# One conformer-attention layer on one core: token tile 0 starts the next stage at both ends, and vector work there in written order

## The chip, the cores and the metric

One core of one Trainium2 chip runs the kernel. The metric is the device time of a whole execution in microseconds (us); lower is better. TensorE is PE in the profile, VectorE DVE, ScalarE ACT, SyncE SP; SP issues every large transfer.

## What is computed

One layer on 256 tokens of 2048 channels, all in float32: a half-step SwiGLU FFN, a token mixing (convolution on one group of channels, differential attention on the other), a second half-step FFN. Each is normalised before and after, and shifted, scaled and gated by nine vectors that are products of a conditioning vector with `w_ada` (2048 x 18432), called adaLN here.

```python
mod = (silu(c) @ w_ada[l] + b_ada[l])
sh1, sc1, gt1, sh2, sc2, gt2, sh3, sc3, gt3 = split(mod, 9)

h = rms_norm(x, g_pre[0]) * (1 + sc1) + sh1
x = x + 0.5 * gt1 * rms_norm(swiglu(h, w_gate1, w_up1, w_down1), g_post[0])

h = rms_norm(x, g_pre[1]) * (1 + sc2) + sh2
u_conv, q, k, v = split(h @ w_in)
y_conv = silu(layer_norm(causal_conv31(glu(u_conv))))
y_attn = rms_norm(diff_attention(q, k, v))
x = x + gt2 * rms_norm(concat(y_conv, y_attn) @ w_out, g_post[1])

h = rms_norm(x, g_pre[2]) * (1 + sc3) + sh3
x = x + 0.5 * gt3 * rms_norm(swiglu(h, w_gate2, w_up2, w_down2), g_post[2])
```

## The kernel before

The 256 tokens are two token tiles of 128 (`NT`), the 2048 channels sixteen chunks of 128 (`NK`, index `kt`). A float32 number is split into a high part that TensorE multiplies exactly and a low part, the rest; every product is three matmuls, high by high, high by low, low by high (`mm3`, L270; blocks of the convolution and of the q and k projections do the same with the weights as the stationary operand).

Weights come in blocks of 1 MB. `load` (L151) issues the transfer on SP's queue into one of four raw buffers, `parts` (L156) makes the high part by a cast on ACT (L160) and the low part by a subtraction on DVE (L162), with three buffers for the results. An adaLN product (`ada_chunk`, L180) is a transfer of 1 MB into the same four raw buffers and one DVE pass over it (L183). There are 144 of them, and they are drawn from a generator (`bg`) wherever the code asks for one: in the fronts of the first FFN, then one for every `EVERY1` weight blocks (`tick`), then in the token mixing and in the front of the second FFN (`late`, one for every `LATE` chunks).

The order of the instructions on each engine is fixed when the kernel is built, by the tile scheduler, except inside a region of `manual_schedule`, where DVE and ACT keep the order in which the code is written (before, that is only the start of the kernel).

The stages in order: four fronts of the first FFN (`MFront`, `first_front`), each cut in four groups of chunks; its remaining gate and up blocks (`wgu`) and down blocks (`wd`); the first end; the convolution's blocks (`Front`, L290), which begin the token mixing; the q and k projections, with the softmax and the convolution's taps (L630) between them; the values (`values`, L718) with the attention products (`mix_values`, L725); the output projection, by heads (`of_heads`) and by convolution channels (`of_conv`); the second end; the second FFN.

An end is where a stage closes. `m_last` (L418) runs the last two units of the output (512 channels each): all products of tile 0, then all of tile 1. `evac` adds the bank to the sum (L486), squares it for the mean (L236) and multiplies by the gate (L489); `close` (L253) normalises the sum, adds it to x (L260) and calls `normed` (L238), which scales x for the next stage (L245 on ACT, L247 on DVE). Then `front_of` (L558) transposes the scaled x chunk by chunk, both tiles at once (`pre_norm`, L212; transposes L218, shift and scale L222 or L225, high part L227, low part L228), and goes on with the next stage's blocks two chunks behind.

The convolution's result is centred and normalised (`center`, L787, `normalize`, L800; L808 sums squares, L811 and L813 invert the root, L818 scales) and split (L173 cast on ACT, L175 subtraction on DVE). The code asks for two adaLN products (`MIXC`) at each of the four output units.

## Time and profile before

| what | value |
|---|---|
| time, median of 3 runs | 1916.03 us (1913.0 to 1920.33) |
| profiled execution, its own time | 1911.84 us |
| its span in the profile | 1910.0 us |
| PE busy | 1836.3 us, 96% |
| DVE busy | 1423.6 us, 75% |
| ACT busy | 821.4 us, 43% |
| DMA | 492.58 MB, mean 258 GB/s |

Times of the trace count from the span's start. A busy share is an average over the stages, which differ: the fronts and the first FFN last to about 774 us, the token mixing to about 1150, the second FFN to the end. The kernel's runs lie within 0.4% of each other.

### The profile page before, as it was taken

The numbers are of one execution on the slowest core, as the hardware profiler recorded it, in microseconds if no ns is written. First come the engines' busy times: TensorE is split into PE (matmuls) and PEld (weight loads), VectorE is DVE, ScalarE is ACT, GpSimd is POOL, SyncE is SP. The second block draws the span as 40 slices with busy tenths as digits, with TensorE's granted clock in tenths as the row PEclk, the third lists the DMA queues.
The fourth block names the chain that finished last, engine by engine and source line by source line (L and its number), as shares of the span: only waits on it lengthen the run. The fifth ranks groups of instructions, "written<-read, shape, count | busy, mean of one in ns | idle before, by whom it ended". The sixth has DMA issues, their size and how long they took to land.

```text
span 1910.0 us, 22064 instructions
## 1 busy us (share of the span) xinstructions
PE 1836.3 (96%) x8944; PEld 1542.5 (81%) x8944; DVE 1423.6 (75%) x1594; ACT 821.4 (43%) x852; POOL 6.0 (0%) x49
## 2 busy tenths in 40 slices
PE   5999999999999999799998897999999999999997
PEld 3788888888888888699997686788888888888886
DVE  7789999788889888688998967854555555555455
ACT  4544445433433334643554454544344333343342
POOL 0000000000000000000000000000000000000000
PEclk9999999999999999899999898999999999999999
DMA  9888877989999998355444665865665666565552
GB/s 362 320 317 330 337 278 290 358 345 361 357 357 370 349 367 323 122 182 185 157 174 157 242 241 202 331 238 205 236 220 205 235 220 226 215 235 210 194 193 72
DMA packets 68934, 492.58 MB, mean 258 GB/s; under 512 B 7648, under 2 KB 7776, under 8 KB 9440
## 3 DMA queue, kind: packets, MB, share of 16 engines
q1 hardware_dynamic: 68832, 491.17, 69.0%
q8 instruction: 70, 1.15, 0.2%
q14 instruction: 32, 0.26, 0.0%
HBM read 489.05 MB, written 2.10 MB: 257 GB/s over the span
## 4 chain that ended last, share of the span: by engine, by line
PE 89%; DVE 5%; ACT 3%; DMA 2%; issue 0%; SPq 0%; DVEq 0%; ACTq 0%
PE ps L273 29%; PE ps L274 29%; PE ps L272 28%; DVE lo L162 2%; DMA raw<-in_wgu 2%; ACT hi L160 1%; DVE raw L183 1%; PE ps L413 1%; ACT tmp L236 1%; PE ps L312 0%; PE ps L311 0%; DMA raw<-in_wk 0%; PE ps L313 0%; PE ps L678 0%; PE ps L218 0%
## 5 line engine op out<-in xcount | busy, mean ns | idle before, releaser
L162 DVE TENSOR_TENSOR lo<-raw,hi 128x2048 fp32r<-128x2048 f32 x314 | 718.5, 2290 | 359.8 <-ACT hi L160 359.1
L160 ACT CAST hi<-raw 128x2048 fp32r<-128x2048 f32 x314 | 600.3, 1912 | 732.4 <-PE ps L274 362.0
L272 PE MATMUL ps<-hi,big 128*128 128x512 f32 x2256 | 879.2, 395 | 16.9 <-ACT big L227 11.3
L273 PE MATMUL ps<-lo,big 128*128 128x512 f32 x2256 | 884.0, 392 | 2.8 <-DVE lo L162 2.8
L274 PE MATMUL ps<-hi,big 128*128 128x512 f32 x2256 | 881.5, 392 | 2.0 <-DVE big L175 1.2
L272 PEld LDWEIGHTS ps<-hi,big 128*128 128x128 f32 x2256 | 426.1, 189 | 106.4 <-ACT big L227 12.7
L273 PEld LDWEIGHTS ps<-lo,big 128*128 128x128 f32 x2256 | 426.5, 189 | 92.5 <-DVE lo L162 6.2
L274 PEld LDWEIGHTS ps<-hi,big 128*128 128x128 f32 x2256 | 425.7, 189 | 92.5 <-DVE big L175 2.5
L183 DVE SCALAR_TENSOR_TENSOR raw<-raw,crow 128x2048 f32<-128x2048 f32 x144 | 327.7, 2283 | 0.6 <-DMA raw<-in_wada 0.5
L272 PE MATMUL ps<-big,hi 128*128 128x256 f32 x448 | 127.3, 284 | 0.0
L273 PE MATMUL ps<-big,hi 128*128 128x256 f32 x448 | 126.7, 283 | 0.0
L274 PE MATMUL ps<-big,lo 128*128 128x256 f32 x448 | 126.7, 283 | 0.0
L630 DVE SCALAR_TENSOR_TENSOR big<-big,par,big 128x256 f32<-128x256 f32 x240 | 100.1, 477 | 0.0
L272 PEld LDWEIGHTS ps<-big,hi 128*128 128x128 f32 x448 | 85.9, 192 | 0.3 <-issue 0.3
L273 PEld LDWEIGHTS ps<-big,hi 128*128 128x128 f32 x448 | 86.0, 192 | 0.0
L274 PEld LDWEIGHTS ps<-big,lo 128*128 128x128 f32 x448 | 85.9, 192 | 0.0
L397 ACT ACTIVATE tmp<-ps 128x256 f32<-128x256 f32 x64 | 24.3, 384 | 96.3 <-PE ps L274 96.3
L486 DVE TENSOR_TENSOR big<-ps,big 128x512 f32<-128x512 f32 x48 | 32.9, 691 | 31.7 <-PE ps L274 31.7
L358 DVE TENSOR_TENSOR big<-ps,big 128x512 f32<-128x512 f32 x72 | 45.2, 681 | 5.4 <-PE ps L274 5.4
L398 DVE TENSOR_TENSOR tmp<-ps,tmp 128x256 f32<-128x256 f32 x64 | 26.1, 421 | 30.9 <-ACT tmp L397 30.9
L218 PE MATMUL ps<-ident,big 128*128 128x128 f32 x96 | 19.7, 297 | 29.6 <-DVE big L247 28.7
L173 ACT CAST big<-ps 128x512 fp32r<-128x512 f32 x44 | 25.8, 585 | 38.0 <-PE ps L413 38.0
(135 smaller groups left out, 742.6 us busy)
## 6 DMA issues: line engine op xcount, KB each, us to landing
raw<-in_wada SPq DMA_DIRECT2D x144, 1024.0 KB, 6.1
raw<-in_wgu SPq DMA_DIRECT2D x116, 1024.0 KB, 5.0
raw<-in_wd SPq DMA_DIRECT2D x88, 1024.0 KB, 5.0
raw<-in_wk SPq DMA_DIRECT2D x60, 1024.0 KB, 5.5
raw<-in_wqk SPq DMA_DIRECT2D x28, 1024.0 KB, 4.8
raw<-in_wo SPq DMA_DIRECT2D x16, 1024.0 KB, 4.8
raw<-in_wv SPq DMA_DIRECT2D x8, 1024.0 KB, 4.8
raw<-in_wkc SPq DMA_DIRECT2D x4, 1024.0 KB, 5.1
```

The lines of the kernel that those rows point to most:

```text
L160: nc.scalar.copy(hi, raw)
L162: ins = nc.vector.tensor_tensor(out=lo, in0=raw, in1=hi.bitcast(F32), op=ALU.subtract)
L173: nc.scalar.copy(hi[:, :w], v[:, :w])
L183: nc.vector.scalar_tensor_tensor(out=raw, in0=raw, scalar=1.0, in1=crow, op0=ALU.mult, op1=ALU.mult, accum_out=acc)
L272: nc.tensor.matmul(o, ah, bh, start=first, stop=False)
L273: nc.tensor.matmul(o, ah, bl, start=False, stop=False)
L274: last_mm[0] = nc.tensor.matmul(o, al, bh, start=False, stop=last)
L358: nc.vector.tensor_tensor(out=a[t], in0=b[t], in1=a[t], op=ALU.add)
L397: nc.scalar.activation(v[:, o], b[t][:, :S], AF.Silu)
L398: nc.vector.tensor_tensor(out=v[:, o], in0=b[t][:, S:], in1=v[:, o], op=ALU.mult)
L486: nc.vector.tensor_tensor(out=y[t][u], in0=b, in1=y[t][u], op=ALU.add)
L630: nc.vector.scalar_tensor_tensor(out=cot(c), in0=vps[c][:, j:j + S], scalar=w, in1=cot(c), op0=ALU.mult, op1=ALU.add)
```

## The change

At both ends the four channel chunks (three at the second end) that the next stage needs first are made for tile 0 alone (`pre_norm_tile`), while tile 1's last products run, and products of the next stage follow at once, first for tile 0, then, when tile 1 is closed, for tile 1. At the first end these are chunks 0 to 3 of both value units, at the second the first eight blocks of the second FFN's front. From the last unit but two of an end up to chunk `FREE` of the next stage DVE and ACT work in written order. adaLN products are spread anew: `BGS` for the fronts (two, two and seven in the second to fourth cut, where there were five in the fourth), `EVERY1` 1.05 and none in the end's group, `LATE` 1.7; four in the token mixing come behind the convolution's last subtraction. The unit `of_heads(3)` moves up, ahead of the convolution's second.

```diff
-EVERY1 = 1.1
+EVERY1 = 1.05
-LATE = 1.4
+LATE = 1.7
+EARLY = 3
+FREE = 6
-LASTC = 3
+BGS = (0, 2, 2, 7)
...
+    def pre_norm_tile(l, xn, h, kts, t, place):
+        b = bank()
+        with tc.issue_after(place.ins):
+            for i, kt in enumerate(kts):
+                nc.tensor.transpose(b[:, i * P:(i + 1) * P], xn[t][kt // 4][:, kt % 4 * P:(kt % 4 + 1) * P], ident)
+        for i, kt in enumerate(kts):
+            two_parts(l, b[:, i * P:(i + 1) * P], h, kt, t * P, P)
...
+    class Lead:
+        def prepare(self):
+            self.pieces = self.open()
+            self.kts = sorted({p[1] for p in self.pieces})
+            self.need(self.kts)
+            self.w = quarters(self.srcs[0])
+            raw = load(self.srcs[1])
+            self.w += [split_act(raw[:, c:c + 512]) for c in range(0, 2048, 512)]
+        def channels(self, xn, t):
+            pre_norm_tile(self.l, xn, self.h, self.kts, t, last_mm[0])
+        def products(self, t):
+            for i, kt, banks, first, last in self.pieces:
+                m_product(banks[t], t, (self.h[kt][:, :S], self.h[kt][:, S:]), self.w[i], first, last)
...
+    class Last:
...
+            if lead:
+                lead.prepare()
+                nc.scalar.activation(small(1, "warm"), csil[:, 0:1], AF.Sqrt, scale=0.0)
+            for u in us:
+                products(0, u)
+                evac(u, 0, self.banks[u][0])
+            xn = [close_(0)]
...
+            for u in us[:-1]:
+                products(1, u)
+            products(1, us[-1], 0, n - EARLY)
+            lead.channels(xn, 0)
+            products(1, us[-1], n - EARLY, n)
+            for u in us:
+                evac(u, 1, self.banks[u][1])
+            lead.products(0)
+            xn.append(close_(1))
+            lead.channels(xn, 1)
+            lead.products(1)
+            return xn
...
-                    if not coming and j % LASTC == LASTC - 1:
+                    for _ in range((j + 1) * BGS[c] // n - j * BGS[c] // n):
                         next(bg)
...
+    h = h1
+    v = {}
+    for u in range(2):
+        for t in range(NT):
+            v[t, u] = big()
+            nc.scalar.copy(v[t, u], vbank[u][t])
...
     def values(u, hooks):
         hacts = [(h[kt][:, :S], h[kt][:, S:]) for kt in range(NK)]
-        banks = m_unit([wv[kq, u] for kq in range(4)], hacts, hooks)
+        banks = m_unit([wv[kq, u] for kq in range(1, 4)], hacts[4:], hooks)
         for t in range(NT):
-            v[t, u] = big()
-            nc.scalar.copy(v[t, u], banks[t])
+            nc.vector.tensor_tensor(out=v[t, u], in0=banks[t], in1=v[t, u], op=ALU.add)
...
+        if u == 0:
+            open_.append(m_unit(of_heads(3), acts, last=False))
+            with tc.issue_after(conv_last[0].ins):
+                for _ in range(2 * MIXC):
+                    next(bg, None)
+    xn = last.run(conv_acts, mix_evac, lambda t: close(t, y, ss, 1.0, False))
```

Three places in the order of the instructions. The first is ACT at the first end, before: L236 are the squares of tile 0's and tile 1's sums and of x, L207 the roots, and `hi_5605` and `hi_5691` casts of the convolution's first weight blocks.

```order
L160 CAST hi_5605<-raw_5603 128x2048
L236 ACTIVATE tmp_5404,ssy_438_2230<-big_2635 128x512
L236 ACTIVATE tmp_5432,ssy_438_2230<-big_2741 128x512
L207 ACT_TABLE_LOAD
L207 ACTIVATE sq_982_5438<-rs_981_5435 128x1
L236 ACTIVATE tmp_5444,ssx_984_5442<-x_81 128x512
L236 ACTIVATE tmp_5447,ssx_984_5442<-x_81 128x512
L160 CAST hi_5691<-raw_5689 128x2048
```

The casts of the next blocks stand between the pieces of closing. The same engine after the change: L231 are the high parts of tile 1's four chunks, L728 the copies of the value banks, and `hi_5753` the cast of the convolution's first block.

```order
L231 CAST big_5603<-tmp_5705 128x128
L231 CAST big_5608<-tmp_5709 128x128
L230 ACTIVATE tmp_5713<-ps_5696,sh,gs 128x128
L231 CAST big_5613<-tmp_5713 128x128
L728 COPY big_5741<-ps_5431 128x512
L728 COPY big_5743<-ps_5432 128x512
L728 COPY big_5745<-ps_5433 128x512
L728 COPY big_5747<-ps_5434 128x512
L165 CAST hi_5753<-raw_5751 128x2048
```

The cast now follows all of closing and the four copies. The second place is DVE while the convolution is normalised, before: L808 and L811 to L818 are the normalisation, L183 the adaLN products with their small L192 and L189, L162 weight subtractions.

```order
L183 SCALAR_TENSOR_TENSOR raw_8773,acc_8775<-raw_8773,crow 128x2048
L808 TENSOR_TENSOR tmp_8607<-tmp_8607,tmp_8612 128x512
L162 TENSOR_TENSOR lo_8702<-raw_8698,hi_8700 128x2048
L808 TENSOR_TENSOR tmp_8607<-tmp_8607,tmp_8615 128x512
L192 SCALAR_TENSOR_TENSOR gs<-acc_8775,par 128x1
L183 SCALAR_TENSOR_TENSOR raw_8778,acc_8780<-raw_8778,crow 128x2048
L811 TENSOR_SCALAR tmp_8621<-ps_8618 128x256
L162 TENSOR_TENSOR lo_8732<-raw_8728,hi_8730 128x2048
L813 RECIPROCAL tmp_8621<-tmp_8621 128x256
```

After the change the same work (L920 to L930, the split L182) stands nearly alone, and the adaLN products (L190) follow it.

```order
L920 TENSOR_TENSOR tmp_8684<-tmp_8684,tmp_8692 128x512
L923 TENSOR_SCALAR tmp_8698<-ps_8695 128x256
L167 TENSOR_TENSOR lo_8799<-raw_8795,hi_8797 128x2048
L925 RECIPROCAL tmp_8698<-tmp_8698 128x256
L930 SCALAR_TENSOR_TENSOR big_6064<-big_6064,par,tmp_8698 128x256 x2
L167 TENSOR_TENSOR lo_8839<-raw_8835,hi_8837 128x2048
L182 TENSOR_TENSOR big_8708<-big_6064,big_8706 128x512
L190 SCALAR_TENSOR_TENSOR raw_8895,acc_8897<-raw_8895,crow 128x2048
L190 SCALAR_TENSOR_TENSOR raw_8900,acc_8902<-raw_8900,crow 128x2048
```

The third place is PE at the first end after the change: `ps_982` is tile 1's last bank, L247 the four transposes of tile 0, and `ps_995` a value bank.

```order
L293 MATMUL ps_982_5398<-hi_987_5407,big_917_5075 128x512
L247 MATMUL ps_1031_5593<-ident_87,big_1027_5546 128x128 x4
L291 MATMUL ps_982_5398<-hi_987_5407,big_916_5073 128x512
L292 MATMUL ps_982_5398<-lo_988_5409,big_916_5073 128x512
L293 MATMUL ps_982_5398<-hi_987_5407,big_917_5075 128x512
L291 MATMUL ps_982_5398<-hi_987_5407,big_943_5234 128x512
L292 MATMUL ps_982_5398<-lo_988_5409,big_943_5234 128x512
L293 MATMUL ps_982_5398<-hi_987_5407,big_944_5236 128x512
L291 MATMUL ps_982_5398<-hi_987_5407,big_943_5234 128x512
L292 MATMUL ps_982_5398<-lo_988_5409,big_943_5234 128x512
L293 MATMUL ps_982_5398<-hi_987_5407,big_944_5236 128x512
L291 MATMUL ps_995_5431<-hi_1000_5437,big_1032_5598 128x512
```

The transposes stand nine matmuls ahead of the end of tile 1's products, and tile 0's value products follow at once; before, the transposes of both tiles stood behind the end.

## Rows read from the trace of the kernel before

**Rows 1.** The page's part 1: busy us, share of the span, instructions.

```profile
PE 1836.3 (96%) x8944; PEld 1542.5 (81%) x8944; DVE 1423.6 (75%) x1594; ACT 821.4 (43%) x852; POOL 6.0 (0%) x49
```

**Rows 2.** Busy by stage: stretch, us, PE, PEld, DVE, ACT, POOL, clock, DMA share, GB/s.

```profile
110.00:240.00 130.00, 130.00 (x582) 107.18 (x581) 122.46 (x129) 52.81 (x40) 0.00 (x0) 1.00 0.87 329
240.00:340.00 100.00, 100.00 (x466) 82.83 (x465) 94.85 (x111) 49.86 (x56) 0.00 (x0) 1.00 0.77 287
340.00:740.00 400.00, 398.93 (x1778) 328.86 (x1777) 340.77 (x311) 153.66 (x108) 0.00 (x0) 1.00 0.94 357
452.00:460.00 8.00, 8.00 (x37) 6.64 (x36) 5.76 (x5) 2.06 (x2) 0.00 (x0) 1.00 1.00 413
...
818.70:1024.83 206.13, 206.13 (x1592) 196.44 (x1591) 189.50 (x349) 94.04 (x135) 3.70 (x32) 1.00 0.49 175
1024.83:1094.47 69.64, 57.52 (x260) 46.43 (x259) 64.61 (x104) 34.11 (x43) 0.00 (x0) 0.90 0.54 199
```

**Rows 3.** Timeline of PE at the first end; the last row from the view of L313.

```profile
768.49 0.39 PE L272 MATMUL ps<-hi,big 128*128 128x512 f32 x1
...
773.70 0.39 PE L274 MATMUL ps<-hi,big 128*128 128x512 f32 x1
...
786.44 0.90 PE L218 MATMUL ps<-ident,big 128*128 128x128 f32 x3 [5.11 <-DVE big L247]
788.14 0.79 PE L311 MATMUL ps<-big,hi 128*128 128x256 f32 x2 [0.79 <-ACT big L227]
...
L313 PE MATMUL ps<-big,lo x64: 278/283/420, 789.0 to 818.3; 128*128 128x256 f32 x64
```

**Rows 4.** The clock behind both ends, columns as in rows 2.

```profile
788.00:792.00 4.00, 3.86 (x18) 3.86 (x19) 1.10 (x3) 1.13 (x4) 0.00 (x0) 0.50 0.00 0
796.00:800.00 4.00, 4.00 (x36) 4.00 (x36) 1.59 (x3) 3.53 (x5) 0.00 (x0) 1.00 0.00 0
...
1162.00:1166.00 4.00, 3.20 (x9) 2.34 (x8) 3.83 (x7) 1.67 (x5) 0.00 (x0) 0.50 0.62 244
```

**Rows 5.** Timeline of DVE at the first end.

```profile
776.33 0.68 DVE L486 TENSOR_TENSOR big<-ps,big 128x512 f32<-128x512 f32 x1
777.03 2.29 DVE L162 TENSOR_TENSOR lo<-raw,hi 128x2048 fp32r<-128x2048 f32 x1
...
781.50 2.74 DVE L260 SCALAR_TENSOR_TENSOR x<-big,ri,x 128x512 f32<-128x512 f32 x4
```

**Rows 6.** Timelines of DVE (first row) and ACT in the token mixing.

```profile
1045.45 0.16 DVE L204 TENSOR_SCALAR rs<-rs 128x8 f32<-128x8 f32 x1
...
1045.23 1.90 ACT L160 CAST hi<-raw 128x2048 fp32r<-128x2048 f32 x1 [3.65 <-PE ps L274]
1047.04 0.20 ACT L207 ACTIVATE sq<-rs 128x8 f32<-128x8 f32 x1
```

**Rows 7.** Timeline of PE in the token mixing: its two long waits' ends.

```profile
1051.05 1.97 PE L760 MATMUL ps<-ident,tmp 128*128 128x128 f32 x8 [5.85 <-DVE tmp L750]
...
1094.47 1.22 PE L274 MATMUL ps<-hi,big 128*128 128x512 f32 x2 [1.24 <-DVE big L175]
```

**Rows 8.** DVE's costliest groups from 1024.83 to 1094.47: count, busy us, mean ns, idle before.

```profile
L162 DVE TENSOR_TENSOR lo<-raw,hi 128x2048 fp32r<-128x2048 f32 x9 | 20.6, 2290 | 4.2 <-ACT hi L160 4.0
L183 DVE SCALAR_TENSOR_TENSOR raw<-raw,crow 128x2048 f32<-128x2048 f32 x6 | 13.7, 2284 | 0.3 <-DMA raw<-in_wada 0.3
L630 DVE SCALAR_TENSOR_TENSOR big<-big,par,big 128x256 f32<-128x256 f32 x32 | 13.7, 474 | 0.0
```

**Rows 9.** Timeline of PE at the second end and in the front behind it.

```profile
1161.41 0.90 PE L218 MATMUL ps<-ident,big 128*128 128x128 f32 x3 [10.90 <-DVE big L247]
1163.11 0.80 PE L272 MATMUL ps<-hi,big 128*128 128x512 f32 x1 [0.80 <-ACT big L227]
...
1219.69 0.50 PE L273 MATMUL ps<-lo,big 128*128 128x512 f32 x1 [1.31 <-DVE lo L162]
```

**Rows 10.** SP's queue of transfers in the first FFN.

```profile
510.53 0.33 SPq L153 DMA_DIRECT2D raw<-in_wgu  x1
...
533.53 3.13 SPq L153 DMA_DIRECT2D raw<-in_wgu  x2
```

More of the change, by code (lines that the diff above doesn't have):

```diff
@@ L210, in rsqrt_tail, with two_parts @@
         return r
+    def two_parts(l, b, h, kt, o, w):
+        if len(h) == kt:
+            h.append(big(F32R))
+        both = h[kt]
+        v = tmp()
+        c = l * NK + kt
+        if l and kt % 2 == 0:
+            nc.vector.tensor_scalar(out=v[:, :w], in0=b, scalar1=gs[:, c:c + 1],
+                                    scalar2=sh[:, c:c + 1], op0=ALU.mult, op1=ALU.add)
+        else:
+            nc.scalar.activation(v[:, :w], b, AF.Identity, bias=sh[:, c:c + 1], scale=gs[:, c:c + 1])
+        nc.scalar.copy(both[:, o:o + w], v[:, :w])
+        last_dve[0] = nc.vector.tensor_tensor(out=both[:, S + o:S + o + w], in0=v[:, :w],
+                                              in1=both[:, o:o + w].bitcast(F32), op=ALU.subtract)
     def pre_norm(l, xn, h, kt):
@@ L288, in s_tile, with add_to @@
         return b
+    def add_to(a, b):
+        nc.vector.tensor_tensor(out=a, in0=b, in1=a, op=ALU.add)
     class Front:
@@ new lines, in block_kernel, with __init__, prepare, run @@
+    ordered = lambda: tc.manual_schedule(engines={mybir.EngineType.DVE, mybir.EngineType.Activation})
+    class Last:
+        def __init__(self, units, lead):
+            self.units, self.lead = units, lead
+            self.region = ordered() if lead else None
+            if lead:
+                self.region.__enter__()
+        def prepare(self):
+            self.ws, self.banks = {}, {}
+            for i, (u, srcs, open_) in enumerate(self.units):
+                self.banks[u] = open_ or [bank() for _ in range(NT)]
+                self.ws[u] = []
+                for s in srcs:
+                    if i == len(self.units) - 1:
+                        self.ws[u] += quarters(s)
+                    else:
+                        raw = load(s)
+                        self.ws[u] += [split_act(raw[:, c:c + 512]) for c in range(0, 2048, 512)]
+        def run(self, acts, evac, close_):
+            lead = self.lead
+            first = {u: open_ is None for u, _, open_ in self.units}
+            us = [u for u, _, _ in self.units]
+            n = len(self.ws[us[0]])
+            def products(t, u, k0=0, k1=n):
+                for k in range(k0, k1):
+                    m_product(self.banks[u][t], t, acts[k], self.ws[u][k], first[u] and k == 0, k == n - 1)
+            if lead:
+                lead.prepare()
[4 more added lines that the diff above has]
+            xn = [close_(0)]
+            if not lead:
+                for u in us:
+                    products(1, u)
+                    evac(u, 1, self.banks[u][1])
+                close_(1)
+                return None
+            for u in us[:-1]:
+                products(1, u)
+            products(1, us[-1], 0, n - EARLY)
+            lead.channels(xn, 0)
+            products(1, us[-1], n - EARLY, n)
+            for u in us:
+                evac(u, 1, self.banks[u][1])
+            lead.products(0)
[3 more added lines that the diff above has]
+            return xn
@@ L485, in evac @@
                     return
+                if not end:
+                    add_to(y[t][u], b)
+                    return
                 nc.vector.tensor_tensor(out=y[t][u], in0=b, in1=y[t][u], op=ALU.add)
@@ L488, in evac @@
                     sum_sq(y[t][u], ss[t][:, u:u + 1])
[L489 to L491 removed]
+                    yg = big()
+                    nc.vector.tensor_tensor(out=yg, in0=y[t][u], in1=gb[u], op=ALU.mult)
+                    y[t][u] = yg
             srcs = lambda u: [wd[c, u] for c in range(f0 // 4, f1 // 4)]
@@ L496, in ffn @@
                     gb[u] = gate_row(l, u)
-                banks = m_unit(srcs(u), acts, tick=tick)
+                    if u == 3 - N_LAST:
+                        last = Last([(w, srcs(w), None) for w in range(4 - N_LAST, 4)], lead)
+                banks = m_unit(srcs(u), acts, tick=(lambda: None) if end else tick)
+                if end and u == 3 - N_LAST:
+                    last.prepare()
                 for t in range(NT):
@@ L502, in ffn @@
                     gb[u] = gate_row(l, u)
-                m_last([(u, srcs(u), None) for u in range(4 - N_LAST, 4)], acts, evac)
-        return xn
+                xn = last.run(acts, evac, lambda t: close(t, y, ss, 0.5, lead is None))
+        return xn, last.region
     done = set()
```

124 lines of the change are left out of this document (52 added, 72 removed).

## The prediction

> **What bounds the kernel now.** I read first the busy shares, then the same shares by stage, then the idle rows of TensorE at the two ends and in the token mixing, and last what VectorE and ScalarE do there. TensorE is busy 96% of the span [rows 1], so 70 us at most can be had by removing idle. By stage [rows 2] it has no idle in the last three fronts of the first FFN (110 to 340), 1.07 us in the 400 us after them, and none from 818.7 to 1024.8. Its idle lies at the first end, in the token mixing and at the second end. The reader should see two kinds of stage: where TensorE is full, vector work is free only while DVE has idle left; where DVE is full (64.6 of 69.6 us from 1024.83 on), a vector operation removed comes back whole.
>
> **First end.** Zero is the end of tile 1's last products, 774.09 [rows 3]. Before, the first matmul of the convolution blocks starts at 788.14: 14.05 us later. Those blocks run to about 818.6, 30.5 us, of which some 3 are lost to the clock: it was granted at 0.50 after this idle, 18 matmuls in 4 us against 36 soon after [rows 4]. So this work ends at zero + 44.6.
>
> Afterwards: 24 products of 512 columns take 23 steps of 5.21/23 us [rows 3], so 5.44 in all; tile 0's eight pieces end at +5.44. DVE goes in written order: tile 0's four channels (their transposes stand nine matmuls, 2.04 us, ahead of zero) take it to +1.95, four evacuations of tile 1 at 0.60 to 0.68 [rows 5] to +4.5, the mean square and root to +5.55. From the residual update to the transposes it is 781.50 to 786.44 [rows 3, 5], 4.94 again: +10.5. From there to the first product it was 1.70 with 256 columns; with half the columns I take 1.3 (an estimate): +11.8, which is 6.4 us of TensorE idle instead of 14.05. Tile 1's pieces take 5.44, and the clock 1.5 (between nothing, as the gap is shorter, and the 3 of before): +18.75. Now ScalarE's order puts four copies of the banks ahead of the next weights' cast, where before casts stood between the pieces of closing. Two of the copies can't start before the last product: 1.2. Then cast 1.90 [rows 6] and subtraction 2.29 [rows 5], so the first product with a low part starts at +18.75 + 5.4. What is left, about 208 of 218 matmuls and transposes at 27.5/218 us, is 26.3, with 1 more for the clock: +51.5. Four more transposes come (0.45). That is 7.4 later than before, but 48 products of the values, 10.9 us, are done: **−3.5**. Bounds: 0 if all of it goes to waits, −11.5 if the weights are ready (4.9 less) and the clock stays up.
>
> On ScalarE's order the trace says: DVE's L204 had given its result at 1045.61, but the 128x8 root (L207) started at 1047.04, after the 1.90 us cast that stood ahead [rows 6]. The Trainium skill, "TensorE: Matmul & The Clock Gate" (the table at its head), has ScalarE's and VectorE's queues as strictly first in, first out, eight deep; the trace agrees, 1.43 us of waiting by a ready instruction. By the rule the cast stays behind the copies and the term is the −3.5 above; could it pass them and run during the pieces, the wait of 5.4 would go and the term be −8.9.
>
> **The values' other half and the convolution.** Of the 10.9 us half leaves values(0), where TensorE had no idle (818.7 to 1024.8) and DVE 16.6 us of it; half leaves values(1) in the stretch 1024.83 to 1094.47 [rows 2], from the first half's attention products to the first product with a low part of the convolution's activations [rows 7]. This stretch is DVE's: 64.6 of 69.6 us busy. It has nine weight subtractions, six adaLN products and 32 taps [rows 8]. After the change the six products (13.7 and their reads, 14.0) wait until the convolution is normalised, one subtraction (2.3) leaves with a value block, and six more taps (0.43 each, 2.5; fewer blocks before it carry taps) and two additions (0.62 each) come: 64.6 − 12.5 = 52.1 of DVE work, and the 5.0 it sat idle stay. I keep 0.8 back for new waits, as head_acts(0) is covered by 24 products instead of 48 and heads(3) comes before the mean: −11.7, 57.9 us. TensorE's wait of 5.85 [rows 7] becomes by this several of 4 to 5, all inside DVE's time. 5.4 of the 11.7 are the values already counted: **−6.3**. Bounds: 0, if the new waits fall on the path or the six products (now behind conv's last subtraction, still due by the second end) delay the next weights; −9.0, if all of it but one block's wait is given back.
>
> **Second end.** Before, TensorE stops at 1150.5, the first product starts at 1163.11 [rows 9]: 12.6. At 0.50 of the clock nine matmuls ran in the next 3 us [rows 4], 1.55 lost, and a stall of 1.31 follows at 1219.69: 15.5. Now banks need no addition, so tile 1's chain is two evacuations shorter: its residual update starts at +3.2 (three channels, two evacuations, the root) and the gap ahead of its pieces is 3.2 + 4.94 + 1.3 − 5.44 = 3.9 or 4.0; clock 1.2. But the transposes of the next channels stand behind tile 1's pieces on TensorE, and the cast of the third weight block behind those channels on ScalarE: 3.3 of waiting (1.4 for transposing and casting, 1.9 for the cast), and its subtraction behind one adaLN product on DVE (2.3 + 2.3, six products in between): 1.6, then 0.7 in small waits and 2.0 for the clock. Sum 12.7: **−2.8**. Bounds 0 and −8 (no clock loss, and the cast early).
>
> **Earlier adaLN, fewer later.** Six more adaLN products run in the fronts: four in 110 to 240, where DVE has 7.5 us idle and they need 4 × 2.36 = 9.4, two in 240 to 340, where 5.15 is enough for 4.7 [rows 2, 8]. TensorE is full there: +2 (0 if the idle suffices; 6 if weights come late as well). In the first FFN's rest one comes every 1.05 blocks and not 1.1. A block is 24 products, 5.53 us as measured (the 400 us hold 1778 matmuls and transposes, 24.6 to a block, so 72.3 blocks); two transfers of 1.05 MB per pair make the demand (1 + 1/1.05) × 1.05/5.53 = 370 GB/s against 362; the stretch moved 357 [rows 2]. SyncE's queue issued four pairs from 510.53 to 533.53, 5.75 each [rows 10]: 20 pairs and one block more take 117.9, 21 blocks 116.1. Over the 76 blocks, three and a half such lots, it would be 6.5, but an 8-us window shows 413, so the pace of that queue isn't the transfers' limit: +1 (0 to 7). Together **+3** (0 to 13).
>
> **Sum.** −3.5 − 6.3 − 2.8 + 3 = −9.6. The profiled execution took 1911.84 (its span and 1.84 around it): 1902.2. It was 4.2 under the median of the runs shown, so the forecast is **1906**.
>
> **Rivals.** (1) Waits hidden: the weights stand ready at both ends and the clock stays at 2.4 GHz. −11.5 − 6.3 − 8 + 3 = −23: **1893**. For it: four raw buffers could be filled during closing, the queue has nothing else. Against: ScalarE's written order. (2) The gain is eaten at the ends and early: the terms of both ends near 0, +3 to +8 early, and the mixing's −6.3: **1913 to 1918**, not measurable. The transfers' form of it: if pairs can't come faster than 5.75, the FFN's 148 transfers take 148 × 2.875 = 425.5 us against 417 of products, +8.5, and 1906 becomes **1913**. Against it are 413 GB/s in 452 to 460 [rows 2]. The Trainium skill, "DMA: Bandwidth & Descriptors" (Where 436 GB/s comes from), gives about 358 GB/s to a core from memory; this stretch's mean of 357 looks like it, the 413 contradicts it for a lone core. By its figure 155 MB would need 433.5 us, an estimate of +16.5 and 1921. (3) Slower: each added early product goes straight into TensorE's path. Where: the fronts and the FFN's rest, ten products (six, and four from the denser ticks) of 2.36, +23.6 in place of +3: **1927**. It decides if DVE's idle of 12.7 us in 110 to 340 can't be used because it lies in pieces between weights; six products need 14.2. (4) The change does nothing at the ends, since the order that was scheduled was as good: the terms for both ends 0, **1913**, counted with (2).
>
> **How the numbers follow.** Chances: forecast 0.42 (1900 to 1911), waits hidden 0.18, eaten 0.26, slower 0.14. A measurement of this kernel tells 0.5%, 9.6 us, from no change, so faster ends at 1906.4 and slower begins at 1925.6. Faster: 0.18 and two thirds of 0.42, 0.46; slower: three quarters of 0.14 and a little of the eaten, 0.14; same: 0.40. The range, 1892 to 1922, leaves out half of the slower case and the far side of the hidden one; the likeliest case's own is 1900 to 1911.
>
> **What would show it.** Right: about 6 us of idle ahead of tile 1's pieces at the first end and 4 at the second; a wait for cast and subtraction of some 5 behind them; the stretch from values(1) to the convolution's products 11 to 12 shorter; the last three fronts up to 2 longer. Wrong: tile 0's transposes late, so that TensorE stops three products before the end; stalls on L167 all through the first FFN; the clock low during both tiles' pieces.

## The result and the profile after

The changed kernel takes 1929.81 us (median of 6, 1924.55 to 1932.25) against 1913.91 (6 runs of before beside it): 1.0076 times as long, interval 1.0056 to 1.0096. The forecast was 1906 in 1892 to 1922, so it lies outside, on the other side. The profiled execution took 1928.92 with a span of 1927.1, 17.1 more than before's 1910.0.

To see where, I cut each span at three marks that every kernel has, each the start of a row: the first multiplication of up by gate out of a bank, which is the first one behind the fronts (L398 on DVE, after the change L425; called the first gate product here), the last matmul of the convolution's blocks (L313, L335), and the first run of the last of the three lines of the attention products (L736, L848). The first mark in the view of a line, before and after, and the second after:

```profile
L398 DVE TENSOR_TENSOR tmp<-ps,tmp x64: 410/424/425, 460.3 to 1854.7; 128x256 f32<-128x256 f32 x64
```

```profile
L425 DVE TENSOR_TENSOR tmp<-ps,tmp x64: 411/424/425, 476.0 to 1873.0; 128x256 f32<-128x256 f32 x64
L335 PE MATMUL ps<-big,lo x64: 281/283/562, 820.7 to 845.1; 128*128 128x256 f32 x64
```

| kernel | to the first gate product, us | to the convolution blocks' end | to attention | to the end | ratio of times to before, interval |
|---|---|---|---|---|---|
| before | 460.3 | 358.0 | 204.4 | 887.3 | |
| changed | 476.0 | 369.1 | 199.9 | 882.1 | 1.0076 (1.0056 to 1.0096) |
| e1 | 461.4 | 367.4 | 199.9 | 895.1 | 1.0077 (1.0046 to 1.0107) |
| e2 | 472.2 | 366.6 | 199.9 | 881.4 | 1.0051 (1.0034 to 1.0067) |
| e3 | 461.5 | 367.5 | 199.9 | 896.7 | 1.0063 (1.0048 to 1.0078) |
| e4 | 478.6 | 359.4 | 204.4 | 887.2 | 1.0071 (1.0056 to 1.0086) |
| e5 | 467.9 | 367.1 | 199.9 | 882.3 | 1.0007 (0.9998 to 1.0016) |
| e6 | 475.2 | 368.6 | 199.9 | 882.1 | 1.0079 (1.0052 to 1.0107) |
| e7 | 471.6 | 364.0 | 199.9 | 878.2 | 1.0041 (1.0023 to 1.0058) |
| e8 | 477.0 | 360.1 | 204.3 | 886.0 | 1.0071 (1.0056 to 1.0086) |
| e9 | 475.1 | 365.7 | 199.9 | 881.4 | 1.0068 (1.0049 to 1.0087) |
| e10 | 460.7 | 366.6 | 199.9 | 893.8 | 1.0065 (1.0043 to 1.0086) |
| e11 | 461.7 | 367.3 | 199.9 | 891.0 | 1.0053 (1.0035 to 1.0071) |
| e12 | 465.1 | 369.5 | 199.9 | 890.5 | 1.0039 (1.0024 to 1.0054) |
| f1 | 462.1 | 371.7 | 199.9 | 883.5 | 1.0008 (0.9995 to 1.0021) |
| f2 | 460.6 | 358.1 | 204.4 | 890.2 | 1.0003 (0.9993 to 1.0012) |
| f5 | 462.1 | 355.4 | 205.1 | 888.9 | 1.0004 (0.9993 to 1.0015) |
| g1 | 472.9 | 367.7 | 199.9 | 882.2 | 1.0059 (1.0036 to 1.0082) |
| g2 | 470.5 | 367.4 | 199.9 | 876.7 | 1.0025 (1.0015 to 1.0035) |

The labels e1 to g2 are the experiments below. Kernels with the same code in a stage agree within 1.6 us in the last two columns (one profile each) and within 7 to 8 in the first two; smaller differences of single profiles there are not read. 15.7 of the 17.1 us are lost ahead of the first gate product. Some 2 of them lie ahead of the first matmul of 512 columns (at 20.6 us before, 22.6 after); no edit touches that part, and it lies anywhere from 20.4 to 23.1 over all profiles.

Busy shares by stage after (columns as in [rows 2]): TensorE, full from 110 to 340 us before, now has 5.56 and 1.75 us of idle there and 5.15 in the 400 us behind; DVE is at 219 of these 230 us, where it had 217.

```profile
110.00:240.00 130.00, 124.44 (x545) 101.85 (x545) 121.58 (x126) 47.08 (x36) 0.00 (x0) 0.99 0.85 324
240.00:340.00 100.00, 98.25 (x455) 81.03 (x455) 97.22 (x118) 49.51 (x57) 0.00 (x0) 1.00 0.79 301
340.00:740.00 400.00, 394.85 (x1741) 320.91 (x1740) 344.83 (x319) 149.97 (x105) 0.00 (x0) 1.00 0.96 362
1047.10:1106.95 59.85, 48.82 (x225) 39.45 (x223) 53.72 (x95) 27.37 (x33) 0.00 (x0) 0.93 0.34 127
1175.10:1183.10 8.00, 7.95 (x24) 6.33 (x25) 1.20 (x4) 0.95 (x3) 0.00 (x0) 0.68 0.00 0
```

The stops of TensorE, from its timeline. The first four belong to the second and third cut of the fronts, as many as the adaLN products that were added there; the next three rows answer to [rows 3], those from 1103.76 to 1108.82 to [rows 7], the rest to [rows 9].

```profile
144.09 0.50 PE L292 MATMUL ps<-lo,big 128*128 128x512 f32 x1 [2.22 <-DVE lo L167]
...
179.32 0.50 PE L292 MATMUL ps<-lo,big 128*128 128x512 f32 x1 [1.82 <-DVE lo L167]
...
215.89 0.50 PE L292 MATMUL ps<-lo,big 128*128 128x512 f32 x1 [1.52 <-DVE lo L167]
...
250.83 0.50 PE L292 MATMUL ps<-lo,big 128*128 128x512 f32 x1 [1.75 <-DVE lo L167]
...
805.35 1.12 PE L247 MATMUL ps<-ident,big 128*128 128x128 f32 x4 [4.42 <-DVE big L266]
807.30 0.79 PE L291 MATMUL ps<-hi,big 128*128 128x512 f32 x1 [0.83 <-ACT big L231]
817.82 0.39 PE L333 MATMUL ps<-big,hi 128*128 128x256 f32 x1 [2.77 <-ACT hi L165]
...
1103.76 0.50 PE L291 MATMUL ps<-hi,big 128*128 128x512 f32 x1 [1.55 <-ACT hi L165]
1106.95 0.79 PE L292 MATMUL ps<-lo,big 128*128 128x512 f32 x1 [2.69 <-DVE lo L167]
...
1108.82 0.63 PE L293 MATMUL ps<-hi,big 128*128 128x512 f32 x1
...
1173.41 0.90 PE L247 MATMUL ps<-ident,big 128*128 128x128 f32 x3 [2.45 <-DVE big L266]
1175.15 0.79 PE L291 MATMUL ps<-hi,big 128*128 128x512 f32 x1 [0.83 <-ACT big L231]
...
1184.17 0.44 PE L239 MATMUL ps<-ident,big 128*128 128x128 f32 x2 [0.44 <-ACT tmp L230]
1185.52 0.44 PE L239 MATMUL ps<-ident,big 128*128 128x128 f32 x2 [0.91 <-DVE tmp L227]
1187.76 2.93 PE L291 MATMUL ps<-hi,big 128*128 128x512 f32 x6 [1.80 <-ACT hi L165]
...
1235.14 0.79 PE L292 MATMUL ps<-lo,big 128*128 128x512 f32 x1 [2.30 <-DVE lo L167]
1243.52 0.50 PE L292 MATMUL ps<-lo,big 128*128 128x512 f32 x1 [1.17 <-DVE lo L167]
```

What DVE does ahead of the first stop, from its timeline: three adaLN passes, then six additions of a front's banks (L310), and only then the subtractions that TensorE waits for; no idle in between.

```profile
130.86 2.29 DVE L190 SCALAR_TENSOR_TENSOR raw<-raw,crow 128x2048 f32<-128x2048 f32 x1
...
133.07 2.29 DVE L190 SCALAR_TENSOR_TENSOR raw<-raw,crow 128x2048 f32<-128x2048 f32 x1
...
135.49 2.28 DVE L190 SCALAR_TENSOR_TENSOR raw<-raw,crow 128x2048 f32<-128x2048 f32 x1
...
138.16 3.67 DVE L310 TENSOR_TENSOR big<-ps,big 128x512 f32<-128x512 f32 x6
141.75 6.68 DVE L167 TENSOR_TENSOR lo<-raw,hi 128x2048 fp32r<-128x2048 f32 x3
```

The same place before, in windows as long as three weight blocks, with two products in each. DVE was busy 16.36 of 16.50 and 16.27 of 16.30 us in the two fullest, 15.16 in the one around the start of the first of these, and four more up to 234 us had 1.06 to 1.36 us idle each. That idle lies in pieces; the longest one from 110 to 240 us is 1.34 us (last row). A pass takes 2.28.

```profile
126.50:143.00 16.50, 16.50 (x75) 13.66 (x74) 15.16 (x17) 6.62 (x5) 0.00 (x0) 1.00 0.83 319
134.40:150.90 16.50, 16.50 (x75) 13.62 (x74) 16.36 (x17) 6.54 (x6) 0.00 (x0) 1.00 0.84 312
150.90:167.20 16.30, 16.30 (x75) 13.44 (x74) 16.27 (x17) 6.36 (x5) 0.00 (x0) 1.00 0.88 343
```

```profile
134.40 0.69 DVE L358 TENSOR_TENSOR big<-ps,big 128x512 f32<-128x512 f32 x1 [1.34 <-PE ps L274]
```

### The profile page after: what moved, and what is told of

The parts are those of the page before. It is cut to its first block, busy times and chain, and to the rows that moved or that the text cites. A ratio compares the mean times of both kernels' runs of the same rounds, so it can differ in the third digit from the quotient of the medians.

```text
span 1927.1 us, 22106 instructions
## 1 busy us (share of the span) xinstructions
PE 1848.8 (96%) x8944; PEld 1545.4 (80%) x8944; DVE 1429.4 (74%) x1615; ACT 822.6 (43%) x870; POOL 6.0 (0%) x49
## 4 chain that ended last, share of the span: by engine, by line
PE 79%; DVE 11%; DMA 5%; ACT 4%; issue 1%; SPq 0%; DVEq 0%; ACTq 0%
PE ps L292 25%; PE ps L293 25%; PE ps L291 25%; DVE lo L167 5%; DMA raw<-in_wgu 2%; ACT hi L165 2%; DMA raw<-in_wd 2%; DVE raw L190 2%; DVE big L310 1%; PE ps L440 1%; DVE big L744 1%; ACT tmp L255 0%; DMA x<-in_x 0%; PE ps L333 0%; PE ps L335 0%
## 5 line engine op out<-in xcount | busy, mean ns | idle before, releaser
L190 DVE SCALAR_TENSOR_TENSOR raw<-raw,crow 128x2048 f32<-128x2048 f32 x144 | 327.5, 2284 | 0.0
L310 DVE TENSOR_TENSOR big<-ps,big 128x512 f32<-128x512 f32 x104 | 66.5, 683 | 8.6 <-PE ps L293 8.6
L424 ACT ACTIVATE tmp<-ps 128x256 f32<-128x256 f32 x64 | 24.2, 384 | 87.9 <-PE ps L293 87.9
L230 ACT ACTIVATE tmp<-ps,sh,gs 128x256 f32<-128x256 f32 (+1 forms) x35 | 19.0, 545 | 88.4 <-PE ps L239 59.2
L425 DVE TENSOR_TENSOR tmp<-ps,tmp 128x256 f32<-128x256 f32 x64 | 25.9, 421 | 24.3 <-ACT tmp L424 23.9
L232 DVE TENSOR_TENSOR big<-tmp,big 128x256 fp32r<-128x256 f32 (+1 forms) x55 | 21.0, 388 | 23.2 <-ACT big L231 23.2
```

What stands on the lines that cost most here:

```text
L190: nc.vector.scalar_tensor_tensor(out=raw, in0=raw, scalar=1.0, in1=crow, op0=ALU.mult, op1=ALU.mult, accum_out=acc)
L232: last_dve[0] = nc.vector.tensor_tensor(out=both[:, S + o:S + o + w], in0=v[:, :w], in1=both[:, o:o + w].bitcast(F32), op=ALU.subtract)
L310: nc.vector.tensor_tensor(out=a, in0=b, in1=a, op=ALU.add)
L424: nc.scalar.activation(v[:, o], b[t][:, :S], AF.Silu)
L425: nc.vector.tensor_tensor(out=v[:, o], in0=b[t][:, S:], in1=v[:, o], op=ALU.mult)
```

## The experiments

**The early products.** The first four undo the fronts' six more products (e1), the denser ticks (e2), both (e3), or make these two alone (e4, on the kernel before).

```diff
-BGS = (0, 2, 2, 7)
+BGS = (0, 0, 0, 5)            # e1, e3
-EVERY1 = 1.05
+EVERY1 = 1.1                  # e2, e3
...
-banks = m_unit(srcs(u), acts, tick=(lambda: None) if end else tick)
+banks = m_unit(srcs(u), acts, tick=tick)   # e2, e3
```

> The changed kernel, with the adaLN products of the fronts as before (five in the fourth cut, none in the second and third); the first FFN's rest keeps one every 1.05 blocks and none in the end's group. Theory E (the denser early products cost the time): the first copy of the down products, 325.4 us before and 335.7 after, comes back to about 328 and the whole to about 1921 us; the 11 us lost between 335.7 and the first end stay. Theory L (the ends' written order or the leading pieces cost the time): no change from 1929.8, within 4 us.

> The changed kernel, with the first FFN's rest as before (one adaLN product every 1.1 blocks, and in the first units of the end's group too); the fronts keep their six more. Theory E: the stretch from the first copy of the down products to the end of the last products of the first end, 448.7 us before and 459.6 after, comes back to about 450, the whole to about 1919 us. Theory L: within 4 us of 1929.8.

> The changed kernel with both early placements as before, so that leads, written order, and the later placement alone are left of the change. Theory E: the first end's last product at 774 to 778 us, the whole 1908 to 1913 us, no slower than before. Theory L: 1925 us or more.

> The kernel before with the early placement alone (two, two and seven products in the fronts, one every 1.05 blocks, none in the end's group). Theory E: 17 to 21 us slower than before, 1931 to 1935 us, less at most 3 for products that have gone from later stages. Theory L: within 5 us of 1914.

Measured 1927.60, 1924.95, 1926.90 and 1928.43 us against 1914.47. e4 alone is as slow as the whole change (less than expected, but theory L is out for it), and without the six products the first gate product is back at 461. But by their whole times e1 and e3 met theory L's numbers, and e2 (six products, 1924.95) met neither: the six that e1 and e3 take out of the fronts then stand in the second FFN's front, fifteen there in place of nine, and the last stage is 13 to 15 us longer. In e4 that front has five in place of eleven and is not shorter (887.2 against 887.3). The denser ticks add no product: up to the convolution's blocks the traces have 109 passes before, in e1 and in e3, 115 in the changed kernel, e2 and e4; and e1 and e3 agree to 0.1 us in the first two stages. They show elsewhere: the kernels that keep the first lead and the ticks as before (e2, e3, e10 to e12, f1, g2) stop for 0.67 (e11) to 3.05 us (f1) ahead of tile 0's transposes at the first end; the others with that lead do not.

**Pass or transfer.** e5 narrows the early products' passes to 128 columns, e6 their transfers to a quarter.

```diff
+w = 128 if light[0] and m >= 2 else 2048                                    # e5
-nc.vector.scalar_tensor_tensor(out=raw, in0=raw, scalar=1.0, in1=crow, ...
+nc.vector.scalar_tensor_tensor(out=raw[:, :w], in0=raw[:, :w], scalar=1.0, in1=crow[:, :w], ...
...
-raw = load(wada[m * NK + kt])
+nc.sync.dma_start(raw[:, :512], wada[m * NK + kt][:, :512])                 # e6
...
```

> The changed kernel, but each of the adaLN products drawn from bg before the convolution's blocks (83 or so, not those of the shift and scale of the first FFN) passes over 128 columns in place of 2048 on DVE; its transfer is whole. Left out: most of those dot products. Theory T (the transfers bind the first FFN; every block more ahead of the first end costs 1.05 MB at some 360 GB/s, 2.9 us): first end's last product stays at 795 us, within 4, the whole within 4 us of the changed kernel's 1929.8. Theory D (DVE binds it): first copy of the down products back from 335.7 to 326 or less, last product back to about 775, the whole 1910 or less. Mixed (DVE in the fronts, transfers after them): first copy near 326, the stretch from it to the last product still some 457 us.

> The changed kernel, but each of those adaLN products transfers a quarter of its block (256 KB), and DVE passes over as many elements as before in two instructions. Left out: three quarters of each weight column. Theory T: last product of the first end back to 770 to 776 us, the whole to about 1908. Theory D: 795 us and 1930, or later by the additional instruction. Mixed: first copy still near 335, the stretch behind it 445 to 449 us in place of 459.6.

1916.24 and 1927.97 against 1915.14. Theory T falls: with 239 GB/s in 340 to 740 in place of 362, e6 takes as long as the changed kernel. e5's whole time is that of before, but with a last stage 5.0 us shorter; ahead of the first gate product it gives 8.1 of the 15.7 us back, and lies between the kernels with five products (460.3 to 465.1) and those with eleven (471.6 to 478.6). TensorE's idle from 110 us to that product is clearer: none before, 9.06 us in the changed kernel, 5.53 in e5, 7.73 in e6. So each edit alone leaves most of the idle. What remains in e5 is a stop every 35 us, at the same places; the last three of its four in the fronts are these.

```profile
175.93 0.50 PE L295 MATMUL ps<-lo,big 128*128 128x512 f32 x1 [1.40 <-DVE lo L167]
210.83 0.50 PE L295 MATMUL ps<-lo,big 128*128 128x512 f32 x1 [1.40 <-DVE lo L167]
245.78 0.50 PE L295 MATMUL ps<-lo,big 128*128 128x512 f32 x1 [1.62 <-DVE lo L167]
```

DVE is busy 262 of 358 us here, so it isn't full. What stands ahead of these stops is a late cast. Before, the cast of the next weight block comes ahead of the shift and scale of a channel chunk (L225). In e5 it comes behind it (L233), and at the changed kernel's four stops too (L230), and that instruction waits some 10.6 us for its transposes; at 136.35 the cast waits for the block's transfer besides. The subtraction then comes behind the additions. ScalarE before, then ScalarE and DVE in e5:

```profile
163.11 1.92 ACT L160 CAST hi<-raw 128x2048 fp32r<-128x2048 f32 x1 [6.79 <-DMA raw<-in_wk]
166.87 0.56 ACT L225 ACTIVATE tmp<-ps,sh,gs 128x256 f32<-128x256 f32 x1 [1.84 <-PE ps L218]
```

```profile
136.35 1.91 ACT L165 CAST hi<-raw 128x2048 fp32r<-128x2048 f32 x1 [1.36 <-DMA raw<-in_wk]
...
168.89 0.56 ACT L233 ACTIVATE tmp<-ps,sh,gs 128x256 f32<-128x256 f32 x1 [10.66 <-PE ps L242]
169.48 0.41 ACT L234 CAST big<-tmp 128x256 fp32r<-128x256 f32 x1
169.79 1.91 ACT L165 CAST hi<-raw 128x2048 fp32r<-128x2048 f32 x1
...
170.52 3.15 DVE L313 TENSOR_TENSOR big<-ps,big 128x512 f32<-128x512 f32 x5
173.59 6.69 DVE L167 TENSOR_TENSOR lo<-raw,hi 128x2048 fp32r<-128x2048 f32 x3
```

So the pass isn't the whole price of an added product. What its transfer and what the new order of cast and subtraction add, no run separates. e6's second instruction adds DVE work (355 of 400 us busy in 340 to 740, 345 in the changed kernel), so it can't say that transfers cost nothing, only that a quarter of them doesn't help.

**Where they stand in the fronts.** e9 moves the draws by two steps, g1 puts all eleven in the fourth cut, f5 takes the five of the kernel before out of the fronts and draws them in the q and k projections.

```diff
-for _ in range((j + 1) * BGS[c] // n - j * BGS[c] // n):
+for _ in range((j + 3) * BGS[c] // n - (j + 2) * BGS[c] // n):   # e9
-BGS = (0, 2, 2, 7)
+BGS = (0, 0, 0, 11)                                              # g1
-LASTC = 3
+LASTC = 99                                                       # f5, on the kernel before
+if hd in (1, 2, 3, 4, 6):
+    next(bg)
```

> The changed kernel, with the fronts' adaLN products drawn two steps off, so that in the second and third cut none stands right behind the two of a channel chunk (the changed kernel has there three transfers in a row in SP's queue). Burst theory (three in a row hold three of the four raw buffers, and the weight block behind them is late): the stalls of 1.5 to 2.3 us on a subtraction near 140, 177, 212 and 247 us go, and the first product of the up blocks' gate (476.0 us in the changed kernel, 460.3 before) comes at 462 to 467; the whole 10 to 13 us faster than the changed kernel. Work theory (six more passes and transfers don't fit, however they lie): 472 or later, and within 4 us of the changed kernel.

> The changed kernel with the same eleven adaLN products of the fronts, but all in the fourth cut, where no channel chunk asks for two of its own. Period theory (in the second and third cut DVE is full: 16.27 of 16.30 us and 16.36 of 16.50 in a period of three weight blocks, so each of the four products there costs its whole pass, 2.4 us; the fourth cut has some 6 us free in each of four periods): first gate product at 463 to 468 in place of 476.0, the whole 8 to 13 us faster than the changed kernel, 1917 to 1922. Plain work theory (six more cost the same in any cut): 473 or later, 1926 or more.

> The kernel before with the five adaLN products of the fourth cut of the fronts drawn in the stage of the q and k projections, where DVE has 16.6 us idle in 206 and the transfers run at half their rate. If a product costs about 2 us wherever DVE is near full (work theory): first gate product at 450 to 453 in place of 460.3, and 0 to 10 us given back in the projections; the whole 1905 to 1914. If front products were free after all: no change, 460.

1926.28, 1925.15 and 1914.08 (before 1913.58, 1914.66, 1914.00). Burst and period theory fall: the first gate product stays at 475.1 and 472.9. The period theory counted some 6 us free in each of four periods of the fourth cut; [rows 2] has 5.15 in all from 240 to 340, and six passes need 14. In g1 the stops have moved with the products, two of 3.0 us in its timeline, and TensorE's idle up to the first gate product is 6.44 us:

```profile
277.29 0.50 PE L292 MATMUL ps<-lo,big 128*128 128x512 f32 x1 [3.02 <-DVE lo L167]
...
315.83 0.80 PE L292 MATMUL ps<-lo,big 128*128 128x512 f32 x1 [3.01 <-DVE lo L167]
```

f5 gives nothing back, 462.1: with five products TensorE is already full there, so fewer don't help. Over six profiles with eleven (changed, e2, e4, e7, e8, e9) the mark is at 475.1 on average, over eight with five (before, e1, e3, e10, e11, e12, f1, f2) at 461.7: 13.4 us for six products, of 2.36 each 14.2. That the two nearly agree is no proof that each costs its pass. Of the changed kernel's 15.7 us only 9.06 are idle of TensorE; some 2 are the start, and the rest are slower steps (behind the stop at 179.32 the granted clock is 0.83 from 180 to 190 us, the lower of its two levels for part of the time). And e5's short passes leave 5.53 of idle. No run has six to ten products.

**The leads.** e7 leaves the second lead out, e8 the first; f1 is the kernel before with the first alone.

```diff
-last = Last([(w, of_conv(w), open_[w]) for w in range(4 - N_LAST, 4)], lead)
+last = Last([(w, of_conv(w), open_[w]) for w in range(4 - N_LAST, 4)], None)      # e7, f1
...
-xn, region = ffn(..., Lead(1, h1, [wv[0, u] for u in range(2)], vlead, needs(1)))
+xn, region = ffn(..., None)                                                      # e8
...
```

> The changed kernel without lead and written order at the second end (both tiles are closed and then transposed together, as before); all else as changed. Theory S (the second lead loses: pieces at the low clock, weight cast and subtraction late behind it): 3 to 6 us faster than the changed kernel, 1924 to 1927. Rival (it gains the 2.8 forecast, and the loss behind it comes from the adaLN products): 1 to 5 us slower, 1931 to 1935.

> The changed kernel without lead and written order at the first end (values of four blocks each in the token mixing, as before); all else as changed. Theory T: two value blocks fewer are transferred ahead of the first end, so its last product comes at about 789.5 in place of 795.3, which pays for the 5.5 us that the lead gained behind it: 1927 to 1933, no change. Rival (the lead's gain is whole): 1934 to 1938.

> The kernel before with the lead and written order at the first end alone: adaLN products of every stage as many and where they were, heads(3) in its old place, no lead at the second end. If the lead is worth nothing net (as e8 against the changed kernel said): 9 us more from the first gate product to the end of the convolution's blocks, 4.4 and some 5 us less behind them, 1912 to 1917, same as before. If it gains by itself what the prediction gave it and half the values in the mixing: 1905 to 1909. If e11's 1923 is the lead's: 1920 or more.

1924.22 and 1928.62 (before 1915.14), 1915.99 (before 1914.00). The second lead costs 3.9 us in its stage, as theory S says; two more pairs that differ by it give 2.8 (e10, e11) and 5.5 (g1 and g2, which differ in the ticks too). The loss does not lie at the end itself. Counted from the first attention product, the changed kernel is 1.8 us ahead of e7 both at TensorE's 480th matmul, ahead of the end, and at the 740th, behind the pieces; at the 800th it is 3.9 behind. Between these lie the stops at 1235.14 and 1243.52, which e7 doesn't have. At the first, two adaLN passes stand ahead of the subtraction, right after 3.95 us in which DVE idled:

```profile
1227.96 0.43 DVE L232 TENSOR_TENSOR big<-tmp,big 128x256 fp32r<-128x256 f32 x1 [3.95 <-ACT big L231]
1228.31 2.28 DVE L190 SCALAR_TENSOR_TENSOR raw<-raw,crow 128x2048 f32<-128x2048 f32 x1
...
1230.52 2.28 DVE L190 SCALAR_TENSOR_TENSOR raw<-raw,crow 128x2048 f32<-128x2048 f32 x1
...
1232.80 2.28 DVE L167 TENSOR_TENSOR lo<-raw,hi 128x2048 fp32r<-128x2048 f32 x1
```

The first lead is worth nothing: from e8 to the changed kernel the second stage grows by 9.0, and the next two shrink by 4.4 and 3.9; from before to f1 it grows by 13.7 for 4.5 and 3.8, and f1's whole time is that of before.

**The mixing and its products.** f2 is the kernel before with the convolution's new order alone. In f2 all eight products of the mixing come behind the convolution's last subtraction, in the changed kernel four. e10 to e12 have fronts and ticks as before and look for a better place for the products left over: one per chunk in the second FFN's front (e10 with both leads, e11 with the first), or eight in the mixing (e12, first lead).

```diff
+if u == 0:                                                     # f2
+    open_.append(m_unit(of_heads(3), acts, last=False))
+    with tc.issue_after(conv_last[0].ins):
+        for _ in range(2 * MIXC):
+            next(bg, None)
...                                                             # two more at each of the next two units
-LATE = 1.7
+LATE = 1.0                                                     # e10, e11; 1.4 in e12
-for _ in range(2 * MIXC):
+for _ in range(4 * MIXC):                                      # e12
```

> The kernel before with heads(3) ahead of the convolution's second unit and its adaLN products of the mixing behind the last subtraction of the convolution (four there, two at each of the next units); no lead at either end, fronts and ticks as before. The prediction's step (six passes leave DVE's chain, 14 us): the stretch from the first half's attention products to the first product with a low part 8 to 12 us shorter than 69.6, the whole 1904 to 1909. Rival (the passes and transfers only move, and the weights behind them come late by as much): 1911 to 1918, and a wait of 4 to 7 us in the output units.

> As e3 (both early placements as before, both leads), but the products left for the second FFN's front are drawn one per chunk (LATE 1.0) and not one per 1.7, so that fewer of the fifteen pile up ahead of the last chunks. From the first attention product to the end e3 took 896.7 us, the changed kernel 882.1, before 887.3. Burst theory: back to 882 to 886, the whole 11 to 14 us faster than e3, 1913 to 1916. Work theory (six more in that front cost their 2.4 us each): 892 or more, the whole 1923 or more.

> The lead at the first end alone (as e7), both early placements as before (as e3), and one product per chunk in the second FFN's front. By the stages of e3 and e7: 461.5 to the first gate product, 366 on to the convolution's blocks' end, 199.9 to the first attention product, and by the burst theory 878 to 882 from there: span 1905 to 1910, time 1908 to 1914, no slower than before. Work theory: 892 from there, 1921 or more.

> As e11, but eight products in the token mixing, all behind the convolution's last subtraction, and eleven in the front at one per 1.4 chunks, as many in each stage as in the kernel before. If the products are hidden in that front (as they are before), no difference to e11 but the passes of four more behind the subtraction: 878 to 890 from the first attention product to the end, 1908 to 1920.

f2: 1914.93 against 1914.00, as the rival said. Its first product with a low part of the convolution's activations (L276, 1091.38) comes 66.2 us after the attention products' end (1025.23) in place of 69.6, 3.5 earlier, but the second FFN's first product at 1166.57, 3.5 later than before [rows 9]. Its timeline shows the waits at the convolution's units and behind the passes:

```profile
1089.51 0.79 PE L275 MATMUL ps<-lo,big 128*128 128x512 f32 x1 [2.29 <-DVE lo L162]
1116.48 0.50 PE L275 MATMUL ps<-lo,big 128*128 128x512 f32 x1 [0.99 <-DVE lo L162]
1129.56 0.73 PE L274 MATMUL ps<-big,big 128*128 128x512 f32 x2 [2.32 <-ACT big L175]
1155.62 0.55 PE L220 MATMUL ps<-ident,big 128*128 128x128 f32 x3 [3.75 <-DVE big L249]
```

e10, e11 and e12: 1925.57, 1923.21 and 1921.28 (before 1913.58); the last stage stays at 893.8, 891.0 and 890.5, so spreading saves 3 us of e3's 15, not all: burst theory falls there too. e12 and f1 have the same lead and as many products in each stage, and differ in the mixing's order: with the new one the last stage is 7.0 us longer (890.5 against 883.5) and the time 1.0039 in place of 1.0008 of before. Its eight passes start from 1100.8 to 1123.1 us, and at 1127.48 TensorE has waited 5.47 us for a weight cast.

**The parts that looked best.** g2 has the first lead, the new order, the ticks as before and the eleven in the fourth cut.

> All that the stages recommend: the lead at the first end alone, the convolution's new order, ticks as before, the eleven products of the fronts all in the fourth cut. By stages: 464 to the first gate product, 364 to the end of the convolution's blocks, 199.9 to the first attention product, 878 from there: span 1906, time 1906 to 1912 by the period theory, faster than before by up to 0.4%. Plain work theory: 1918 or more.

1920.38 against 1914.66, slower still, as plain work theory said. No complete version run here beats the kernel before; f1, f2 and f5 equal it.

## Why the prediction was wrong

**Earlier adaLN, +3: wrong, 13 to 16.** The step that failed is "four in 110 to 240, where DVE has 7.5 us idle and they need 4 × 2.36 = 9.4", priced at +2. It set the products against the sum of DVE's idle over 130 us. That idle couldn't be had: it lay in pieces of 1.34 us at most, and TensorE was full too, so each of the four made a stop of 1.52 to 2.22 us. Rival (3), that each early product goes straight into TensorE's path, had the condition (idle in pieces) and nearly the time, 1927; I gave it 0.14. In the time there is luck: it counts 9.4 us for four products of the denser ticks, which do not exist (109 passes with either), and takes gains at both ends that did not come. As to the mechanism, the pass of 2.36 is only one of two parts; e5 shows that passes of 128 columns leave 5.53 of 9.06 us of idle. Its rows put that down to late weights and their order on ScalarE, which no run tests, and how the two share the loss stays open.

**Transfers, rival (2).** By the rule of the Trainium skill, "DMA: Bandwidth & Descriptors" (Where 436 GB/s comes from), some 358 GB/s would bind the first FFN, whose stretch moved 357 before and 362 after. The trace of e6 disagrees as to what binds: two thirds of that rate took the same time. From 340 to 740 us TensorE is busy 398.9 of 400 us before and 394.9 after, so little time was there to be had from transfers.

**First end, −3.5: the chain was right, the balance not.** Tile 1's first product came 11.8 us after the end of tile 1's last of the stage before (795.49; forecast 11.8), the first with a low part of the weights at +25.2 (24.2), the blocks' end at +49.9 (51.9) against 44.5: 5.4 later, for 10.9 us of values done. ScalarE's order held, as the prediction had it: in its timeline the copies stand ahead of the cast, and TensorE waits 2.77 us.

```profile
814.41 1.56 ACT L728 COPY big<-ps 128x512 f32<-128x512 f32 x3 [4.32 <-PE ps L293]
815.85 1.92 ACT L165 CAST hi<-raw 128x2048 fp32r<-128x2048 f32 x1
```

So against before the term came out at −5.5 behind its zero. Two things took it back. Against e8, which lacks this lead alone, the blocks' end behind zero is 6.7 later, and the next two stages give 8.3 of the 10.9 back (4.4 and 3.9). And from the first gate product to zero the changed kernel takes 2.3 us more than e8, f1 2.9 more than before. The failed step is that the term put the time ahead of zero at nothing without a reason, though two value blocks more are transferred, cast and subtracted there. That these loads are the 2 to 3 us is argued, not shown; single profiles differ by as much in that stage.

**The mixing, −6.3: two thirds of the stretch, and not the sum.** To the same product, the first with a low part of the convolution's activations (1108.82), the stretch is 61.7 us in place of 69.6, 7.9 shorter where I took 11.7, of which 5.4 are the values; by the new order alone it is 3.5 (f2). What stands in its place are waits of 1.55 and 2.69 for a cast and a subtraction at the convolution's first products, for which I kept 0.8. Behind the stretch the products that moved (four, 9.4 us of passes; eight in f2 and e12) stand ahead of the subtractions and evacuations. By itself the order takes back all of the 3.5 and 3 more (f2: 204.4 + 890.2 against 204.4 + 887.3), and 7.0 in e12. The step that failed is "a vector operation removed comes back whole", read for one stretch: the operation was not removed. The bound of 0 named this case.

**Second end, −2.8: nothing at the end, and a loss behind it that the term did not have; +3.9 (e7 against the changed kernel).** The gap ahead of tile 1's pieces was 4.2 (3.9) and the waits behind them 3.2 (4.9 and 0.7). The pieces ran 8.0 us in place of 5.44 at a mean clock of 0.68, 2.5 lost where I took 1.2. Up to there the lead neither gains nor loses against e7. The step that failed is that the front behind runs on as before: the two stops of 2.30 and 1.17 at 1235 and 1243, the first with the clock at 0.83 behind it, make a difference of 5.7 against e7, of which 1.8 is what the changed kernel had ahead.

**Chances.** 0.14 for slower by over 0.5% was low, since the early term and the mixing's rest on the same premise, that DVE has room for a pass put elsewhere.

## What to carry to other kernels

Look not only at how much idle an engine has, but at how long its pieces are: 7.5 us idle in 130, in pieces of 1.34 us at most, did not hold four passes of 2.36. Where TensorE is full and the idle of DVE comes in such pieces, moving a pass from one such stage to another was no gain here: six passes of 2.36 cost 13.4 us where they went, and taking five away gave nothing. Look at the weight block behind an added transfer too, since here its cast and subtraction came late. Count the loads of a piece that leads where they are fetched, not only its products where they are multiplied. Measure a stretch to the same product in both kernels.

## What the runs showed that I had not expected

A quarter of the adaLN bytes changes nothing in a stretch that looks bound by transfers at 0.96 DMA share (e6: 239 GB/s against 362, same time). Passes of 128 columns in place of 2048 leave more than half of the idle that the six products made (e5: 5.53 of 9.06 us). And the fronts are lopsided: six products more cost 13.4 us, five fewer give nothing (475.1, 461.7, 462.1 at the same mark).
